# Seven block products in place of eight for the gate and value of the second block's FFNs

## The chip, the cores and the metric

The kernel runs on one core of one Trainium2 chip. The metric is the device time of one execution in microseconds, the median of several runs. TensorE (PE) multiplies, VectorE (DVE), ScalarE (ACT) and GpSimd (POOL) do elementwise work, and SyncE (SP) issues the loads of the weights.

## The reference, cut to what matters

Two blocks run one after the other on 512 tokens of 1024 channels, all in fp32. The first block (three mixers and a convolutional FFN) is not touched. The second block has a SwiGLU FFN ahead of its mixer and one behind it, and only these two are changed:

```
def swiglu(x, w_gate, w_up, w_down):
    return (jax.nn.silu(x @ w_gate) * (x @ w_up)) @ w_down

x = x + 0.5 * swiglu(rms_norm(x, ffn1_norm), ffn1_w_gate, ffn1_w_up, ffn1_w_down)
x = x + token_mixer(...)
x = x + 0.5 * swiglu(rms_norm(x, ffn2_norm), ffn2_w_gate, ffn2_w_up, ffn2_w_down)
```

The hidden width is 2816, which is 22 tiles of 128 channels.

## The kernel before

Activations lie with channels on the 128 partitions and the 512 tokens along the free dimension. A product of fp32 accuracy is made of three fp32r products: each operand is cut into a high part (ACT copies it with rounding, `whi`, `uh`, `hh`) and a low part (DVE subtracts, `wlo`, `ul`, `hl`), and PE adds up high by high, high by low and low by high (`dense`, L284).

All weights come in one stream, in tiles of 128 x 1024 fp32 (512 KB), in the order of use. `Weights.next` (L266 to L276) takes one: a load on SP's queue into `raw` (three buffers), the cut on ACT into `whi` (L273) and on DVE into `wlo` (L274), three buffers each.

In an FFN of the second block (`ffn2`, `glu`), a hidden tile j takes two weight tiles, gate and value. Each is eight input blocks of 128 by 128 against 512 tokens: 8 x 3 = 24 matmuls with a moving operand of 512 columns, so 48 for the two. The right side is `us`, x times the norm's vector and cut; the norm's factor by token, `R`, is multiplied in behind the product: `gg` = product x R (DVE), silu (ACT), x R (POOL, L1487), x value product (DVE, `gh`), then the cut into `hh` and `hl`. An FFN works in two halves of 11 hidden tiles, each followed by its part of the product with `w_down` (`down`), which adds into x (`xa` in the first FFN, `xb` in the second, called f1 and f2 here).

The products have six PSUM buffers (`mm`). The first three products of an FFN are made together by `first`, while x is still being finished. `R` comes from row sums on PE (`nst`), a power on POOL (`rr`), a spread by transposes on PE (`nbc`) and a copy on ACT (`R`).

The scheduler of the language sets the order of the instructions on each engine; each engine then works strictly in that order, waiting on semaphores.

Of the kernel before, what the change touches and what calls it, by code (L numbers as in the profile page):

```python
# [18 lines left out]
P = 128  # L19
T = 512  # L20
# [235 lines left out]
class Weights:  # L256
# [3 lines left out]
        self.nc, self.pool, self.src, self.raw_bufs, self.bufs = nc, pool, src, raw_bufs, bufs  # L260
        self.i = 0

    def next(self, label, e=None):
        nc, i = self.nc, self.i
        lab, bl = PLAN[i]
        assert lab == label, (lab, label)  # L266
        n = sum(len(c) for _, _, c in bl)
        raw = self.pool.tile([P, 1024], F32, name="raw", bufs=self.raw_bufs)
        nc.sync.dma_start(raw[:, :n], self.src[i][:, :n])
        w = raw[:, :n]  # L270
        hi = self.pool.tile([P, 1024], F32R, name="whi", bufs=self.bufs)
        lo = self.pool.tile([P, 1024], F32R, name="wlo", bufs=self.bufs)
        nc.scalar.activation(hi[:, :n], w, AF.Copy)  # L273
        (e or nc.vector).tensor_tensor(lo[:, :n], w, hi[:, :n].bitcast(F32), op=ALU.subtract)  # L274
        self.i += 1
        return hi, lo  # L276


# [1 line left out]
def two_blocks(ctx, tc, ins, out):  # L280
    nc = tc.nc
    S, V, G, PE = nc.scalar, nc.vector, nc.gpsimd, nc.tensor
# [24 lines left out]
    W = Weights(nc, wpool, ins["wst"], 3, 3)  # L307
# [28 lines left out]
    st = ctx.enter_context(tc.tile_pool(name="st", bufs=1))  # L336

    def tmp(name="tmp"):
        return st.tile([P, T], F32, name=name, tag="tmp", bufs=3)

    ALL = slice(0, T)
    HALVES = (slice(0, T // 2), slice(T // 2, T))
# [39 lines left out]
        return R  # L382

    class SqSum:
        def __init__(self, pool=None):
            self.acc = (pool or st).tile([P, T], F32, name="acc")
            self.new = {0, T // 2}

        def add(self, ap, e=V, s=ALL):
# [56 lines left out]
    part = big.tile([P, 8, T], F32, name="part")  # L446
# [5 lines left out]
    blk = ExitStack()  # L452
# [70 lines left out]
    with tc.tile_pool(name="lin", bufs=1) as lin, tc.tile_pool(name="p0", bufs=1, space=PSUM) as p0:  # L523
# [19 lines left out]
        mps, ws = [None] * 8, [None] * 8  # L543
# [66 lines left out]
    def pm():  # L610
        return bank("m", nm[0])
# [681 lines left out]
    R = st.tile([P, T], F32, name="R")  # L1293
# [64 lines left out]
    blk = ExitStack()  # L1358
    psm = blk.enter_context(tc.tile_pool(name="psm2", bufs=6, space=PSUM, reuse_waits="tile"))
    psx = blk.enter_context(tc.tile_pool(name="psx", bufs=2, space=PSUM, reuse_waits="tile"))  # L1360
    fp = blk.enter_context(tc.tile_pool(name="fp", bufs=1, reuse_waits="tile"))

    def pm():
        return psm.tile([P, T], F32, name="mm")
# [112 lines left out]

    k2, ka0, ka1, ka2 = sk

    def glu(label, R):  # L1480
        def hidden(j):
            pg = up(label)
            pv = up(label)
            g = fp.tile([P, T], F32, name="gg", bufs=3)
            tt(g, pg, R, MUL)
            act(g, g, AF.Silu)
            G.tensor_tensor(g, g, R, op=MUL)  # L1487
            h = fp.tile([P, T], F32, name="gh", bufs=2)
            tt(h, pv, g, MUL)
            return h  # L1490
        return hidden

    def ffn2(label, R, q):

        hidden = glu(label + "_up", R)
        for h in range(2):
            hs = []
            for j in range(11 * h, 11 * h + 11):
                t = hidden(j)
                a = fp.tile([P, T], F32R, name="hh", bufs=14)  # L1500
                b = fp.tile([P, T], F32R, name="hl", bufs=14)
# [43 lines left out]
    R = rms_bcast(pss, "pO", rn)  # L1545
# [123 lines left out]
    def pair(q, k, place):  # L1669

        h, l = parts(q, stage("h"), stage("l"))
        qs = [place("qa"), place("qb")]
        for s, o in enumerate(((h, l), (l, h))):
            for i in range(2):
                hand(qs[s][H2[i]], o[i][H2[s]])
        h, l = parts(k, stage("h"), place("kl"))
        ks = [place("ka"), place("kb")]
        for s, t in enumerate(ks):
            for i in range(2):
                hand(t[H2[i]], h[H2[s]])  # L1680
        return [(a, b, l) for a, b in zip(qs, ks)]
# [120 lines left out]
    with tc.tile_pool(name="cc", bufs=1, reuse_waits="tile") as cc:  # L1802
# [29 lines left out]
        for j in range(2):  # L1832
# [6 lines left out]
            for i in range(NB):  # L1839
                n = (i + 1) * P  # L1840
# [31 lines left out]
    ps = pT()  # L1872
# [178 lines left out]
```

## Time and profile before

| | |
|---|---|
| median of 3 runs | 2189.31 us (2188.54 to 2191.35) |
| the profiled execution | 2191.79 us, of which the span is 2190.0 us |
| PE busy, of the span | 97% |
| DVE, ACT, POOL busy | 52%, 36%, 23% |
| f1: from the first `gg` to the last add into `xa` | 935.3 to 1263.8 us |
| f2: from the first `gg` to the last add into `xb` | 1851.4 to 2186.3 us |

Times in the rows are microseconds from the start of the span. An engine's busy time is a union of its instructions; matmuls overlap each other, so the pace of PE is read from the distance of their starts, not from their durations. A number in square brackets behind a row is the engine's idle time ahead of it, with what ended it. "PEclk" is the granted TensorE clock as a share of full speed.

### The profile page before, as it was taken

The numbers are of one execution on the slowest core, as the hardware profiler recorded it, in microseconds if no ns is written. First come the engines' busy times: TensorE is split into PE (matmuls) and PEld (weight loads), VectorE is DVE, ScalarE is ACT, GpSimd is POOL, SyncE is SP. The second block draws the span as 40 slices with busy tenths as digits, with TensorE's granted clock in tenths as the row PEclk, the third lists the DMA queues.
The fourth block names the chain that finished last, engine by engine and source line by source line (L and its number), as shares of the span: only waits on it lengthen the run. The fifth ranks groups of instructions, "written<-read, shape, count | busy, mean of one in ns | idle before, by whom it ended". The sixth has DMA issues, their size and how long they took to land.

```text
span 2190.0 us, 31626 instructions
## 1 busy us (share of the span) xinstructions
PE 2132.7 (97%) x12492; PEld 1758.9 (80%) x12492; DVE 1145.0 (52%) x2158; ACT 787.1 (36%) x1330; POOL 513.5 (23%) x549
## 2 busy tenths in 40 slices
PE   7988999998999999899999999999999999999999
PEld 5877777666788888788888889998877888888887
DVE  6653445668652564643344439967554455433442
ACT  4422223553442443332222325445443233222221
POOL 3168661234000000321011023343121022100110
PEclk9988998998999999999999999999999999999999
DMA  8244334101452222222222343342252222222222
GB/s 309 100 137 155 118 132 135 52 11 45 160 176 98 99 99 97 68 95 97 97 97 96 124 147 107 94 139 78 104 151 77 97 96 96 97 96 96 97 97 86
DMA packets 84846, 238.31 MB, mean 109 GB/s; under 512 B 13970, under 2 KB 21448, under 8 KB 84570
## 3 DMA queue, kind: packets, MB, share of 16 engines
q1 hardware_dynamic: 78874, 226.19, 31.1%
q0 software_dynamic: 5104, 9.52, 1.2%
q8 instruction: 98, 1.61, 0.3%
q10 hardware_dynamic: 720, 0.57, 0.1%
q14 instruction: 50, 0.41, 0.1%
HBM read 216.02 MB, written 15.33 MB: 106 GB/s over the span
## 4 chain that ended last, share of the span: by engine, by line
PE 87%; POOL 4%; DMA 4%; DVE 3%; issue 1%; ACT 1%; SPq 0%; POOLq 0%; DVEq 0%; ACTq 0%
PE mm L284 67%; PE psm L284 4%; PE pS L284 3%; PE psr L284 2%; DMA raw<-in_ada_dram 2%; POOL am L634 2%; PE pO L284 2%; PE pss L284 2%; PE k L284 2%; PE pso L284 1%; POOL raw L633 1%; PE pT L1636 1%; PE pst L1097 1%; DMA raw<-in_wst_dram 1%; DVE ul L299 1%
## 5 line engine op out<-in xcount | busy, mean ns | idle before, releaser
L273 ACT ACTIVATE whi<-raw 128x1024 fp32r<-128x1024 f32 (+4 forms) x314 | 327.8, 1046 | 828.1 <-PE mm L284 608.5
L274 DVE TENSOR_TENSOR wlo<-raw,whi 128x1024 fp32r<-128x1024 f32 (+4 forms) x302 | 371.4, 1231 | 345.0 <-ACT whi L273 341.1
L284 PE MATMUL mm<-ul,whi 128*128 128x512 f32 (+1 forms) x1296 | 502.1, 388 | 6.0 <-DVE ul L299 6.0
L284 PE MATMUL mm<-uh,wlo 128*128 128x512 f32 (+1 forms) x1296 | 501.7, 388 | 1.0 <-DVE wlo L274 1.0
L284 PE MATMUL mm<-uh,whi 128*128 128x512 f32 (+1 forms) x1296 | 496.4, 388 | 4.3 <-ACT uh L287 3.3
L284 PEld LDWEIGHTS mm<-ul,whi 128*128 128x128 f32 x1296 | 245.1, 189 | 58.7 <-DVE ul L299 8.7
L284 PEld LDWEIGHTS mm<-uh,whi 128*128 128x128 f32 x1296 | 243.5, 190 | 55.4 <-ACT uh L287 4.7
L284 PEld LDWEIGHTS mm<-uh,wlo 128*128 128x128 f32 x1296 | 245.2, 189 | 51.1 <-DVE wlo L274 1.9
L284 PE MATMUL mm<-hh,wlo 128*128 128x512 f32 (+1 forms) x550 | 209.3, 381 | 0.0
L284 PE MATMUL mm<-hl,whi 128*128 128x512 f32 (+1 forms) x550 | 209.3, 381 | 0.0
L284 PE MATMUL mm<-hh,whi 128*128 128x512 f32 (+1 forms) x550 | 208.4, 381 | 0.0
L1487 POOL TENSOR_TENSOR gg<-gg,R 128x512 f32<-128x512 f32 x44 | 77.4, 1761 | 473.4 <-ACT gg L287 473.4
L284 PE MATMUL mm<-whi,uh 128*128 128x256 f32 (+1 forms) x488 | 140.5, 288 | 0.0
L284 PE MATMUL mm<-whi,ul 128*128 128x256 f32 (+1 forms) x488 | 139.8, 287 | 0.0
L284 PE MATMUL mm<-wlo,uh 128*128 128x256 f32 (+1 forms) x488 | 139.2, 285 | 0.0
L284 PEld LDWEIGHTS mm<-hl,whi 128*128 128x128 f32 x550 | 103.4, 188 | 19.9
L284 PEld LDWEIGHTS mm<-hh,whi 128*128 128x128 f32 x550 | 103.4, 188 | 19.8
L284 PEld LDWEIGHTS mm<-hh,wlo 128*128 128x128 f32 x550 | 103.4, 188 | 19.5
L287 ACT ACTIVATE p<-p,smin 128x128 f32<-128x128 f32 (+4 forms) x136 | 81.8, 602 | 91.8 <-DVE smin L1073 56.2
L290 DVE TENSOR_TENSOR gh<-mm,gg 128x512 f32<-128x512 f32 x44 | 30.4, 691 | 130.8 <-PE mm L284 125.2
L284 PEld LDWEIGHTS mm<-whi,ul 128*128 128x128 f32 x488 | 93.2, 191 | 1.7 <-issue 1.5
L284 PEld LDWEIGHTS mm<-whi,uh 128*128 128x128 f32 x488 | 93.0, 191 | 1.4 <-issue 0.4
(520 smaller groups left out, 3415.4 us busy)
## 6 DMA issues: line engine op xcount, KB each, us to landing
raw<-in_wst_dram SPq DMA_DIRECT2D x294, 512.0 KB, 3.2
raw<-in_ada_dram SPq DMA_DIRECT2D x32, 512.0 KB, 6.3
aw<-in_ada_dram SPq DMA_DIRECT2D x16, 512.0 KB, 8.5
raw<-in_wst_dram SPq DMA_DIRECT2D x8, 448.0 KB, 7.4
ka<-d POOLq DMA_DIRECT2D x1, 3570.0 KB, 49.9
k<-d POOLq DMA_DIRECT2D x1, 2556.0 KB, 20.8
part<-in_x_dram SPq DMA_DIRECT2D x4, 512.0 KB, 6.3
xa<-in_x_dram SPq DMA_DIRECT2D x8, 256.0 KB, 4.6
```

The lines of the kernel that those rows point to most:

```text
L273: nc.scalar.activation(hi[:, :n], w, AF.Copy)
L274: (e or nc.vector).tensor_tensor(lo[:, :n], w, hi[:, :n].bitcast(F32), op=ALU.subtract)
L284: PE.matmul(o, l, r, start=start, stop=stop)
L287: S.activation(o, i, f, **kw)
L290: V.tensor_tensor(o, a, b, op=op)
L299: V.scalar_tensor_tensor(o, a, s, b, op0=op0, op1=op1)
L633: G.tensor_scalar(aw[:, r], aw[:, r], s, 1.0, op0=MUL, op1=MUL)
L634: G.tensor_tensor(am, am, aw[:, r], op=ADD)
L1097: PE.transpose(ps[:, j:j + P], p[:, j:j + P], ident)
L1487: G.tensor_tensor(g, g, R, op=MUL)
L1636: PE.transpose(ps[:, j:j + P], p[:, o + j:o + j + P], ident)
```

## The change

Hidden tiles 0 to 2 of each FFN stay as they were. For tiles 3 to 21 the two weight tiles and the tokens are seen as two by two blocks: the left matrix has rows gate and value and columns channels 0 to 511 and 512 to 1023 (a11, a12, a21, a22, each 128 x 512 as stored); the right one has rows of channels and columns of tokens 0 to 255 and 256 to 511. Seven products of sums of blocks give the four blocks of outputs, where eight products of blocks did it before. One such product is 4 channel blocks x 3 = 12 matmuls with 256 moving columns; seven are 84.

- `Sevenths.make`, once for each FFN, builds the seven right sides for 4 channel blocks, cut into high and low (`th`, `tl`). It now takes R into them: 8 multiplications of 128 x 512 on DVE (`ta`, `tb`), 8 subtractions of 128 x 256 on POOL, 8 on DVE, 12 copies on ACT and 12 subtractions on DVE (256, 512 and 1024 wide). It works in two buffers in `part` (`stage`).
- `pair`, once for each of the 19 tiles, loads the two weight tiles, makes four sums of 128 x 512 on POOL (L1535 to L1538) into the same `stage` buffers, cuts three tiles of 1024 and one of 512 (`w4`), runs the products into three PSUM buffers (two of them are read by ACT or DVE part of the way and added to later), and makes up the outputs with five 256-wide operations on DVE and one addition on POOL (L1564), copies and silu on ACT. The last product of a tile (`rest`) is put behind the first of the next tile (`settle`).
- A `raw` buffer is now free for its next load when POOL's sums, ACT's copies and DVE's subtractions have all read it. In the built program the second weight tile of every pair (`w2`) gets the same one of the three buffers, and the first tiles (`w1`) take the other two by turns. `w2` is read by L1535 and L1537 on POOL, by ACT's copy into `w4h` and by DVE's subtraction into `w4l`, and on DVE's queue this `w4l` stands behind the two multiplications `gg<-gg,part` that finish the tile two before it.
- The buffers for `hh` and `hl` (14 each) become six and the free `us` slots; `gg` lies in a shared buffer.

```
+        def product(self, ps, a, c, which, start=False, stop=False):
+            for k in range(4):
+                ah, al = [w[:, c * T + k * P:c * T + k * P + P] for w in a]
+                bh, bl = [w[:, which] for w in self.t[k]]
+                for i, (l, r) in enumerate(((ah, bh), (ah, bl), (al, bh))):
+                    PE.matmul(ps, l, r, ...)
...
+        def pair(self, label, j, use):
+            w1, w2 = W.load(label), W.load(label)
+            a11, a12, a21, a22 = w1[:, :T], w1[:, T:], w2[:, :T], w2[:, T:]
+            s12, s34 = self.stage
+            G.tensor_tensor(s12[:, :T], a21, a22, op=ADD)
+            G.tensor_tensor(s12[:, T:], s12[:, :T], a11, op=SUB)
+            G.tensor_tensor(s34[:, :T], a11, a21, op=SUB)
+            G.tensor_tensor(s34[:, T:], a12, s12[:, T:], op=SUB)
+            wa, ws, wd = W.cut(w1), W.cut(s12), W.cut(s34)
+            wb = [fp.tile([P, T], F32R, name="w4" + c, bufs=2) for c in "hl"]
+            act(wb[0], a22, AF.Copy)
+            tt(wb[1], a22, wb[0].bitcast(F32), SUB)
...
+            self.product(pa_, wa, 0, 4, True)
+            act(s1, pa_, AF.Copy)
+            self.settle()
+            self.product(pb_, ws, 1, 1, True)
+            tt(u2, pb_, s1, ADD)
+            self.product(pc_, ws, 0, 0, True)
+            act(s5, pc_, AF.Copy)
+            self.product(pa_, wa, 1, 5, stop=True)
+            act(g[:, A], pa_, AF.Silu)
+            self.product(pb_, wd, 0, 2)
+            tt(u3, pb_, s1, ADD)
+            self.product(pc_, wd, 1, 6, stop=True)
+            tt(g[:, B], pc_, u2, ADD)
+            act(g[:, B], g[:, B], AF.Silu)
+            G.tensor_tensor(s5, s5, u3, op=ADD)
+            def rest():
+                self.product(pb_, wb, 0, 3, stop=True)
+                tt(s1, pb_, s1, ADD)
+                tt(g[:, B], g[:, B], s5, MUL)
+                tt(g[:, A], g[:, A], s1, MUL)
+                use(g)
+            self.owed = rest
...
     def ffn2(label, name, R, q, seven):
         hidden = glu(label + "_up", R)
+        seven.make(name, R)
         for h in range(2):
...
             for j in range(11 * h, 11 * h + 11):
+                if j < S0:
+                    use(hidden(j))
+                else:
+                    seven.pair(label + "_up", j, use)
```

At the start of f1, DVE's queue before the change goes from the spread of the norm (`rv`, `rb`) at once to the first `gg`, with the weights' cuts between:

```order
L294 TENSOR_SCALAR rv<-nst 128x4
L373 COPY rb<-rr 128x512
L274 TENSOR_TENSOR wlo<-raw,whi 128x1024
L290 TENSOR_TENSOR gg<-mm,R 128x512 x3
L290 TENSOR_TENSOR gh<-mm,gg 128x512
```

The same queue after the change, the last twelve rows up to the first `gg`; `ta`, `tb` and `part` are `make`'s operands, `tl` the low cuts of the right sides:

```order
L305 SCALAR_TENSOR_TENSOR tb<-xa_4300,vec,R 128x512
L296 TENSOR_TENSOR part<-tb,part 128x256
L296 TENSOR_TENSOR tl_8449<-part,th_8448 128x1024
L296 TENSOR_TENSOR tl_8453<-ta,th_8452 128x256
L305 SCALAR_TENSOR_TENSOR ta<-xa_4297,vec,R 128x512
L296 TENSOR_TENSOR tl_8453<-tb,th_8452 128x512
L296 TENSOR_TENSOR tl_8451<-part,th_8450 128x1024
L296 TENSOR_TENSOR part<-tb,part 128x256
L296 TENSOR_TENSOR tl_8455<-ta,th_8454 128x256
L305 SCALAR_TENSOR_TENSOR tb<-xa_4301,vec,R 128x512
L296 TENSOR_TENSOR part<-tb,part 128x256 x2
L296 TENSOR_TENSOR gg<-mm,R 128x512
```

Between `rb` and the first `gg` there now stand 24 instructions of `make`: 8 of form `ta` or `tb`, 11 of 128 x 256, 3 of 128 x 512 and 2 of 128 x 1024; behind this `gg` come a subtraction of 256, a cut of 512, a `gg` and a cut of 1024. The first block product stands on PE 12 matmuls (all 512 wide) behind `nbc` in f1 and 40 behind it in f2, and needs a PSUM buffer that the first `gg` frees, since tiles 0 to 2 hold all six.

On POOL, before the change, the queue of f1 holds one multiplication for each hidden tile:

```order
L396 TENSOR_TENSOR acc<-acc,sq 128x512 x7
L362 TENSOR_TENSOR rr<-rv,mhalf 128x4
L1487 TENSOR_TENSOR gg<-gg,R 128x512 x22
L274 TENSOR_TENSOR wlo<-raw,whi 128x1024 x3
L362 TENSOR_TENSOR rr<-rv,mhalf 128x4
```

After the change these five rows repeat, tile after tile (the sixth is the next tile's first); the addition L1564 belongs to a tile two before that of the sums around it:

```order
L1535 TENSOR_TENSOR part<-raw 128x512
L1564 TENSOR_TENSOR part<-part 128x256
L1536 TENSOR_TENSOR part<-part,raw 128x512
L1537 TENSOR_TENSOR part<-raw 128x512
L1538 TENSOR_TENSOR part<-raw,part 128x512
L1535 TENSOR_TENSOR part<-raw 128x512
```

POOL thus has four 512-wide and one 256-wide operation for a tile, where it had one of 512.

## Rows read from the trace of the kernel before

**Rows 1.** The page: engines' busy time, and the chain that ended last by engine.

```profile
PE 2132.7 (97%) x12492; PEld 1758.9 (80%) x12492; DVE 1145.0 (52%) x2158; ACT 787.1 (36%) x1330; POOL 513.5 (23%) x549
...
PE 87%; POOL 4%; DMA 4%; DVE 3%; issue 1%; ACT 1%; SPq 0%; POOLq 0%; DVEq 0%; ACTq 0%
```

**Rows 2.** Windows of f1, two hidden tiles; columns: stretch, us, busy by engine, PEclk, DMA.

```profile
937.00:947.88 10.88, 10.88 (x49) 9.01 (x48) 7.85 (x10) 5.18 (x8) 6.43 (x4) 1.00 0.23 78
947.88:958.76 10.88, 10.88 (x49) 9.01 (x48) 4.44 (x5) 3.19 (x4) 1.81 (x1) 1.00 0.35 116
```

**Rows 3.** Timeline of PE, 256-column matmuls at 882.7 us; columns: start, us, instruction.

```profile
882.72 0.28 PE L284 MATMUL mm<-hh,wlo 128*128 128x256 f32 x1
882.84 0.28 PE L284 MATMUL mm<-hh,whi 128*128 128x256 f32 x1
...
883.80 0.28 PE L284 MATMUL mm<-hh,wlo 128*128 128x256 f32 x1
```

**Rows 4.** Timelines of POOL and DVE, 918 to 928 us, both engines on SBUF operands.

```profile
919.25 2.15 POOL L396 TENSOR_TENSOR acc<-acc,sq 128x512 f32<-128x512 f32 x1
918.10 6.62 DVE L274 TENSOR_TENSOR wlo<-raw,whi 128x1024 fp32r<-128x1024 f32 x3 [2.79 <-ACT whi L273]
926.49 1.23 DVE L274 TENSOR_TENSOR wlo<-raw,whi 128x1024 fp32r<-128x1024 f32 x1 [1.77 <-ACT whi L273]
```

**Rows 5.** Timelines of POOL and DVE at 1854.7 us; the DVE operation reads PSUM.

```profile
1854.66 1.30 POOL L1487 TENSOR_TENSOR gg<-gg,R 128x512 f32<-128x512 f32 x1
1854.73 0.69 DVE L290 TENSOR_TENSOR gh<-mm,gg 128x512 f32<-128x512 f32 x1 [2.03 <-POOL gg L1487]
```

**Rows 6.** Timelines of ACT and PE: `R`, and `nbc` with the matmul behind it, f1 and f2.

```profile
934.69 0.60 ACT L287 ACTIVATE R<-nbc 128x512 f32<-128x512 f32 x1 [2.10 <-PE nbc L376]
934.41 0.47 PE L284 MATMUL mm<-uh,whi 128*128 128x512 f32 x1
1850.78 0.60 ACT L287 ACTIVATE R<-nbc 128x512 f32<-128x512 f32 x1 [0.97 <-PE nbc L376]
1850.50 0.48 PE L284 MATMUL mm<-uh,wlo 128*128 128x512 f32 x1
```

**Rows 7.** Timeline of DVE: 512-wide with three operands, and 256-wide operations.

```profile
519.11 0.74 DVE L299 SCALAR_TENSOR_TENSOR tmp<-xa,gf,R 128x512 f32<-128x512 f32 x1
519.77 0.74 DVE L299 SCALAR_TENSOR_TENSOR xa<-tmp,sg,xa 128x512 f32<-128x512 f32 x1
906.20 0.41 DVE L1457 TENSOR_TENSOR tmp<-part,R 128x256 f32<-128x256 f32 x1
906.53 0.96 DVE L299 SCALAR_TENSOR_TENSOR ul<-xa,vec,uh 128x256 fp32r<-128x256 f32 x1
908.21 0.47 DVE L299 SCALAR_TENSOR_TENSOR ul<-xa,vec,uh 128x256 fp32r<-128x256 f32 x1
```

**Rows 8.** Timeline of POOL: 256-wide, and two 512-wide that follow each other.

```profile
906.42 0.80 POOL L1457 TENSOR_TENSOR tmp<-part,R 128x256 f32<-128x256 f32 x1 [0.43 <-DVE xa L299]
936.76 1.29 POOL L1487 TENSOR_TENSOR gg<-gg,R 128x512 f32<-128x512 f32 x1 [7.50 <-ACT gg L287]
938.02 1.30 POOL L1487 TENSOR_TENSOR gg<-gg,R 128x512 f32<-128x512 f32 x1
```

**Rows 9.** Groups by line of f1, 937 to 1278 us; columns: xcount, busy us, mean ns, idle before.

```profile
L274 DVE TENSOR_TENSOR wlo<-raw,whi 128x1024 fp32r<-128x1024 f32 x58 | 71.5, 1233 | 45.7 <-ACT whi L273 45.7
L273 ACT ACTIVATE whi<-raw 128x1024 fp32r<-128x1024 f32 x61 | 64.7, 1061 | 214.4 <-PE mm L284 195.1 <-issue 18.8 <-ACT uh L287 0.6
L1487 POOL TENSOR_TENSOR gg<-gg,R 128x512 f32<-128x512 f32 x22 | 39.1, 1781 | 233.5 <-ACT gg L287 233.5
L290 DVE TENSOR_TENSOR hl<-gh,hh 128x512 fp32r<-128x512 f32 x22 | 15.6, 708 | 0.0
L290 DVE TENSOR_TENSOR gg<-mm,R 128x512 f32<-128x512 f32 x20 | 13.8, 690 | 49.2 <-PE mm L284 49.2
```

**Rows 10.** DMA issues of f1, 936 to 1200 us: count, size, median us to landing.

```profile
raw<-in_wst_dram SPq DMA_DIRECT2D x48, 512.0 KB, 3.1
```

**Rows 11.** Windows around the start of f1, where PE waits; columns as in rows 2.

```profile
888.00:891.00 3.00, 0.71 (x7) 0.47 (x5) 2.11 (x4) 1.63 (x3) 1.19 (x1) 1.00 0.53 175
891.00:902.00 11.00, 8.31 (x39) 7.96 (x40) 10.06 (x23) 3.74 (x8) 3.74 (x5) 0.53 0.15 48
```

More of the change, by code (lines that the diff above doesn't have):

```diff
@@ L261, in __init__, with load @@
         self.i = 0
-    def next(self, label, e=None):
+    def load(self, label):
         nc, i = self.nc, self.i
@@ L269, in next, with cut @@
         nc.sync.dma_start(raw[:, :n], self.src[i][:, :n])
-        w = raw[:, :n]
+        self.i += 1
+        return raw[:, :n]
+    def next(self, label, e=None):
+        return self.cut(self.load(label), e)
+    def cut(self, w, e=None):
+        nc, n = self.nc, w.shape[-1]
         hi = self.pool.tile([P, 1024], F32R, name="whi", bufs=self.bufs)
@@ L274, in next @@
         (e or nc.vector).tensor_tensor(lo[:, :n], w, hi[:, :n].bitcast(F32), op=ALU.subtract)
-        self.i += 1
         return hi, lo
@@ L384, in two_blocks, with __init__ @@
     class SqSum:
-        def __init__(self, pool=None):
-            self.acc = (pool or st).tile([P, T], F32, name="acc")
+        def __init__(self, pool=None, tag=None):
+            self.acc = (pool or st).tile([P, T], F32, name="acc", **(dict(tag=tag, bufs=2) if tag else {}))
             self.new = {0, T // 2}
@@ L1360, in two_blocks @@
     psx = blk.enter_context(tc.tile_pool(name="psx", bufs=2, space=PSUM, reuse_waits="tile"))
-    fp = blk.enter_context(tc.tile_pool(name="fp", bufs=1, reuse_waits="tile"))
+    fp0 = ExitStack()
+    fp = fp0.enter_context(tc.tile_pool(name="fp", bufs=1, reuse_waits="tile"))
     def pm():
@@ L1478, in two_blocks, with __init__, make, settle @@
     k2, ka0, ka1, ka2 = sk
+    S0 = 3
+    class Sevenths:
+        def __init__(self):
+            fp.tile([P, 16], F32, name="pad0")
+            self.t = [[fp.tile([P, 7, 256], F32R, name=f"t{c}{k}") for c in "hl"] for k in range(4)]
+            fp.tile([P, 48], F32, name="pad1")
+            self.stage = [part[:, 4 * i:4 * i + 2].rearrange("p a b -> p (a b)") for i in range(2)]
+            self.snap = [[part[:, 4 * i + 2 + c // 2, c % 2 * 256:c % 2 * 256 + 256] for c in range(4)] for i in range(2)]
+            self.owed = None
+        def make(self, name, R):
+            A, B = HALVES
+            for k in range(4):
+                ta, tb = tmp("ta"), tmp("tb")
+                stt(ta, x[k], vc(name, k), R, MUL, MUL)
+                stt(tb, x[k + 4], vc(name, k + 4), R, MUL, MUL)
+                t = self.stage[k % 2].rearrange("p (a b) -> p a b", b=256)
+                G.tensor_tensor(t[:, 0], ta[:, B], ta[:, A], op=SUB)
+                G.tensor_tensor(t[:, 2], tb[:, B], ta[:, B], op=SUB)
+                tt(t[:, 1], tb[:, B], t[:, 0], SUB)
+                tt(t[:, 3], tb[:, A], t[:, 1], SUB)
+                h, l = self.t[k]
+                b2 = tb.rearrange("p (a b) -> p a b", b=256)
+                for i, v in ((slice(4, 5), ta[:, None, A]), (slice(5, 7), b2), (slice(0, 4), t)):
+                    act(h[:, i], v, AF.Copy)
+                    tt(l[:, i], v, h[:, i].bitcast(F32), SUB)
+        def product(self, ps, a, c, which, start=False, stop=False):
+            for k in range(4):
+                ah, al = [w[:, c * T + k * P:c * T + k * P + P] for w in a]
+                bh, bl = [w[:, which] for w in self.t[k]]
+                for i, (l, r) in enumerate(((ah, bh), (ah, bl), (al, bh))):
+                    PE.matmul(ps, l, r, start=start and k == i == 0, stop=stop and k == 3 and i == 2,
+                              skip_group_check=True)
+        def settle(self):
+            if self.owed:
+                self.owed()
+                self.owed = None
+        def pair(self, label, j, use):
[10 more added lines that the diff above has]
+            tt(wb[1], a22, wb[0].bitcast(F32), SUB)
+            n = slice(0, 256)
+            A, B = HALVES
+            s1, s5, u2, u3 = self.snap[j % 2]
+            g = tmp("gg")
+            pa_ = pm()[:, n]
+            self.product(pa_, wa, 0, 4, True)
+            act(s1, pa_, AF.Copy)
+            self.settle()
+            pb_ = pm()[:, n]
+            self.product(pb_, ws, 1, 1, True)
+            tt(u2, pb_, s1, ADD)
+            pc_ = pm()[:, n]
+            self.product(pc_, ws, 0, 0, True)
[15 more added lines that the diff above has]
+            self.owed = rest
@@ L1483, in hidden @@
             pv = up(label)
-            g = fp.tile([P, T], F32, name="gg", bufs=3)
+            g = tmp("gg")
             tt(g, pg, R, MUL)
@@ L1487, in hidden, with ffn2, use @@
             G.tensor_tensor(g, g, R, op=MUL)
-            h = fp.tile([P, T], F32, name="gh", bufs=2)
-            tt(h, pv, g, MUL)
-            return h
+            tt(g, pv, g, MUL)
+            return g
         return hidden
-    def ffn2(label, R, q):
+    def ffn2(label, name, R, q, seven):
         hidden = glu(label + "_up", R)
+        seven.make(name, R)
         for h in range(2):
             hs = []
[L1498 to L1501, printed above, removed]
+            def use(t):
+                j = 11 * h + len(hs)
+                i = j - 6 if j < 14 else j - 17 if j > 19 else -1
+                if i < 0:
+                    a, b = [fp.tile([P, T], F32R, name="hh" if c == "h" else "hl", bufs=6) for c in "hl"]
+                else:
+                    a, b = two(i)
                 act(a, t, AF.Copy)
@@ L1504, in ffn2 @@
                 hs.append((a, b))
+            for j in range(11 * h, 11 * h + 11):
+                if j < S0:
+                    use(hidden(j))
+                else:
+                    seven.pair(label + "_up", j, use)
+            seven.settle()
             def done(m, ps, s):
@@ L1512, in two_blocks @@
     first("f1_up", halves=HF, e=V)
-    q = SqSum(fp)
+    fp0.close()
+    fp = blk.enter_context(tc.tile_pool(name="fp1", bufs=1, reuse_waits="tile"))
+    seven = Sevenths()
+    q = SqSum(fp, "w4h")
     for k in range(8):
@@ L1523, in f1_done @@
             nc.sync.dma_start(xd[m], x[m])
-    ffn2("f1", R, f1_done)
+    ffn2("f1", "f1n", R, f1_done, seven)
     blk.close()
@@ L2000, in two_blocks @@
     fp = blk.enter_context(tc.tile_pool(name="fp4", bufs=1, reuse_waits="tile"))
+    seven = Sevenths()
     first("f2_up", lambda *a: raw("f2n", *a))
     R = rms_bcast(psx, "px", rms_rows(psx, "px", q.acc))
-    ffn2("f2", R, lambda m, s: nc.sync.dma_start(out[m], x[m]))
+    ffn2("f2", "f2n", R, lambda m, s: nc.sync.dma_start(out[m], x[m]), seven)
     blk.close()
```

## The prediction

> **What bounds the kernel now.** The page comes first: PE is busy for 97% of the span and carries 87% of the chain that ended last [rows 1], so time is gained where PE does less, and lost where PE is made to wait. The second view is the windows of the changed stretch: one hidden tile takes 10.88 us, PE is busy in all of it at the full granted clock, and the others have room (second window: DVE 4.44, ACT 3.19, POOL 1.81) [rows 2]. 10.88 over 48 matmuls is 0.2267 us for one of 512 columns. The third is the timeline at the end of the first block's FFN, where matmuls of 256 columns run with nothing in between: nine of them in 1.08 us, 0.120 each [rows 3]. A half-wide matmul thus costs 53% of a full one, not 50%.
>
> **PE's work.** A changed tile takes 84 x 0.120 = 10.08 us in place of 10.88: 0.80 saved, and 38 x 0.80 = 30.4 us for 19 tiles in each FFN, if PE never waits. The Trainium skill, "TensorE: Matmul & The Clock Gate", section "Back-to-back issue gap", gives 518 and 262 cycles for these two widths; by that estimate the saving would be 1.19 us a tile, 45 in all. The rows decide here.
>
> **What POOL and DVE do to each other.** Three cuts `wlo` beside POOL's additions took 6.62 us, 2.21 each, where one alone took 1.23; the addition in between took 2.15 where two in a row start 1.26 apart [rows 4, 8]. 2.21 is about one of each after the other: they take turns. A DVE operation that reads PSUM took 0.69 beside a POOL operation of 1.30, so nothing was added to either [rows 5]. I therefore let every DVE operation on two SBUF operands and every POOL operation exclude each other. What a cut of 1024 adds to POOL's path is 2.21 - 1.26 = 0.95; for 512 I take half, 0.47, for 256 a quarter, 0.24 (estimates). The Trainium skill, "SBUF — State Buffer", section "Who interferes with whom", has this as a rule: a DVE instruction with two SBUF inputs contends with a GpSimd instruction that reads SBUF, and whoever starts first blocks the other. It speaks against this change, and the rows agree with it; without it the sum is that of the third rival.
>
> **A tile in the steady state.** The second weight tiles use one buffer, so a loop goes round once a tile: load 3.1 [rows 10], POOL's four sums 4 x 1.26 = 5.04 and its 256-wide addition 0.80 [rows 8], and DVE operations that get their turn in between: one `wlo` 0.95, the two multiplications that stand ahead of `w4l` 0.48, and `w4l` itself 0.47, behind which the load may start. The sum is 10.84. That is above PE's 10.08 and almost the old 10.88: such a tile gains 0.04. PE should be seen waiting for the 256-wide addition on PSUM that stands behind `w4l` on DVE. Lower end: if `w4l` gets its turn before POOL's fourth sum, the loop is 9.6 and PE's 10.08 holds. Upper end: one more `wlo` in POOL's path, 11.79. I take the middle, since all four sums stand without a gap in POOL's queue. I count 5 tiles of an FFN at PE's pace (three in the first half, whose loads have a lead or whose waits are counted below; two in the second, loaded during `down`), 14 in the loop: 5 x 0.80 + 14 x 0.04 = 4.6 us gained, 9.2 for both.
>
> ACT has by `pair` three copies of 1024 at 1.06 [rows 9] and about 3 us of small ones in a tile, 6 of 10: no bound. Its copies stay in the shade, unless a cut waits for a buffer.
>
> **The start of each FFN.** `make` can't begin before R. On DVE 25 instructions stand from there to the first `gg`, which frees the PSUM buffer for the first block product: 8 x 0.66 (their starts in a row), 11 x 0.33, 3 x 0.63, 2 x 1.15 and 0.69 [rows 7, 9], the starts of the last three forms taken 0.08 before the end of the one ahead, as in rows 7: 13.8 us. POOL's eight subtractions take their turns in between; one of them stretched a DVE operation from 0.47 to 0.96 [rows 7], so 8 x 0.49 = 3.9. Together 17.7 (13.8 if they exclude nothing).
>
> In f1, R is done at 935.3 and PE then has 12 matmuls of 512 from 934.4, to 937.1 [rows 6]. The first block product comes at 935.3 + 17.7 = 953.0: PE idles 15.9 us. In f2, R is done at 1851.4, PE has 40 matmuls from 1850.5 to 1859.6 [rows 6], the product comes at 1869.1: 9.5 idle.
>
> Then the first tile's sums. They need the buffer that `make` still reads: from the first `gg` on DVE 0.33 + 0.63 + 0.61 + 1.15 = 2.7 us. On POOL the sum L1535, a `gg`, L1537 and L1536 follow, 4 x 1.26, with one cut of 1024 and two of 512 taking turns, 0.95 + 0.94; then ACT's copy 1.06: 10.7 in all, of which PE fills 24 x 0.12 = 2.9. Idle: 7.8 us. After that DVE owes five cuts of 1024 beside POOL's sums, 2.21 each, where a product takes PE 1.44: 5 x 0.77 = 3.9.
>
> So f1 loses 15.9 + 7.8 + 3.9 = 27.6, f2 21.2: 48.8. Nothing hides it; before the change the multiplication by R stood behind the products and PE ran on.
>
> **The clock.** Where PE waited at 888 to 891 us (busy 0.71 of 3.0), the granted share was 0.53 from 891 to 902, the 1.2 GHz level for most of it [rows 11]. Idle stretches of 8 to 16 us should do the same. What of such a stretch falls into waiting costs nothing; at worst all 11 us are work at half pace, 5.5 lost for each FFN. I take 3 each, 6.
>
> **Sum.** +48.8 - 9.2 + 6 = +45.6 us. The profiled execution took 2191.8 (span 2190.0), so it would become 2237.4; the median lies 2.5 below it. On the median, 2189.3 + 45.6 = 2235 us, slower by 2.1%.
>
> **Rivals.**
> - The loop is heavier: one more `wlo` in POOL's path makes 11.79 of the 10.84, and 28 tiles x 0.95 = 26.6: 2262. For it: DVE has three `wlo` in every tile. Against: during the 3.1 us of the load POOL does nothing, and two of them fit there.
> - The loop doesn't bind: `w4l` wins its turn. All 38 tiles at PE's pace: 2189.3 + 48.8 + 6 - 30.4 = 2214. For it: PE's tile order leaves the queues room for 2.9 us between the products concerned; against: rows 4, where POOL came back after each single cut.
> - Not slower: POOL's and DVE's operations here don't exclude each other, since other operands lie in other places than in rows 4. Then the start is 13.8 long, PE idles 12.0 and 5.6, then 2.7 + 5.0 + 1.06 - 2.9 = 5.9 in each, nothing for the cuts: 29.4 against 30.4 saved, 2188. That is the tie; idle under 26 us in all would make it faster by over 0.2%. For it: rows 5 show that the exclusion depends on where operands lie. Against: rows 4 are the same forms on SBUF tiles of other names.
> - The change not doing what it says: the scheduler could have left PE's order as it was. The program's order shows 84 matmuls of 256 for a tile, so I give it nothing.
>
> **How the numbers follow.** Forecast 72%, heavier loop 11%, loop not binding 9%, no exclusion 8%. The forecast's own range is 2216 to 2256: 11 us for `make` and the first sums (8 x 0.49 twice, and 1.5 for each start), 6 for the clock. The range for 8 in 10 reaches up past the heavier loop to 2266 and down below the lighter to 2209, and leaves out the tie. A measurement of this kernel can tell about 0.2%, 4.4 us, from no change. Faster by more: 0.03, from the tie's lower side; within it 0.04; slower 0.93.
>
> **What would show it.** In the profile after: an idle PE of some 16 us behind the norm in f1 and 9 in f2, both ended by DVE (a `gg` or a low cut of `make`), then one of some 8 ended by ACT's `whi<-part`; half clock close by; tiles at 10.8 us with one wait of 0.7 or so in each; `wlo` with a mean well above 1.23, and POOL's sums above 1.26. If the tiles run at 10.1, the loop was wrong; if the first idle is under 10 in f1, the start was; if `wlo` stays at 1.23, the exclusion.

## The result

The changed kernel takes 2248.0 us (2246.68 to 2249.87) against 2188.93 (2188.41 to 2191.35) before: a ratio of 1.0268, 95% interval 1.025 to 1.0286. It is slower by 59 us; forecast were 46, with 2235 us in a range of 2209 to 2266.

The profiled execution took 2247.27 us, its span 2245.5. The two lines of the page that stood in [rows 1]: PE's busy share fell from 97% to 94%. The second line can't be set beside the 87% of before as it stands: the chain is followed back only to 911.7 us here, and its shares add up to 60% of the span. Of that stretch (1330 us) the chain lies on PE for 69%, where from 912 us on it was 98% before; "issue" and DVE have about a tenth each now, the DMA and POOL a twentieth each.

```profile
PE 2109.4 (94%) x13860; PEld 1799.3 (80%) x13860; DVE 1385.8 (62%) x2442; ACT 886.0 (39%) x1544; POOL 736.7 (33%) x717
...
PE 41%; issue 6%; DVE 6%; DMA 3%; POOL 3%; ACT 1%; POOLq 0%; SPq 0%; DVEq 0%; ACTq 0%
```

PE is busy for 2109 us, 23 less than before, and yet the span is 55 longer: the work fell and the waiting grew. From the end of `R` to the last add into x, f1 went from 329.2 to 361.1 us and f2 from 335.6 to 362.1, together +58.4; what lies between them is unchanged (586.9 and 587.3). So the whole loss sits in the two changed stretches. The span grew by 55 and not by 58.4 because `R` of f1 was done 3.3 us earlier in this execution (931.96 in place of 935.28); in the profiles of the variants below that time lies anywhere from 931.6 to 936.6.

**The start.** The timeline of PE, the matmuls with the longest idle times ahead of them and a short one, f1 and then f2. Before, PE did not wait at this place at all [rows 6].

```profile
950.02 0.55 PE L1523 MATMUL mm<-th,whi 128*128 128x256 f32 x1 [15.93 <-DVE gg L296]
...
962.17 0.58 PE L1523 MATMUL mm<-th,whi 128*128 128x256 f32 x1 [5.94 <-ACT whi L280]
963.84 0.58 PE L1523 MATMUL mm<-th,wlo 128*128 128x256 f32 x1 [0.45 <-DVE wlo L281]
1898.90 0.55 PE L1523 MATMUL mm<-th,whi 128*128 128x256 f32 x1 [10.02 <-DVE gg L296]
...
1911.72 0.58 PE L1523 MATMUL mm<-th,whi 128*128 128x256 f32 x1 [5.97 <-ACT whi L280]
```

The first idle stretch ends with the first `gg` on DVE, behind `make`; the second with ACT's copy of the first summed weight tile. In f1, `R` is done at 931.96, and DVE's queue then shows 17.2 us of `make` without a hole up to that `gg`:

```profile
931.99 0.75 DVE L305 SCALAR_TENSOR_TENSOR ta<-xa,vec,R 128x512 f32<-128x512 f32 x1 [4.46 <-ACT R L293]
...
948.00 1.28 DVE L296 TENSOR_TENSOR part<-tb,part 128x256 f32<-128x256 f32 x2
949.20 0.68 DVE L296 TENSOR_TENSOR gg<-mm,R 128x512 f32<-128x512 f32 x1
```

The windows behind it show the granted clock (PEclk, third from the end of a row; the first two rows are means over stretches at both levels). Where PE works from 950 to 966 us, the granted share is 0.50 and the half-wide matmuls start 0.21 us apart, the 1.2 GHz level; then 0.118.

```profile
949.20:960.00 10.80, 5.74 (x24) 5.27 (x24) 10.70 (x14) 5.90 (x10) 9.01 (x6) 0.66 0.00 0
960.00:971.00 11.00, 7.96 (x49) 7.47 (x50) 10.14 (x7) 5.19 (x7) 9.68 (x6) 0.72 0.30 95
971.00:982.00 11.00, 10.02 (x86) 9.84 (x84) 8.34 (x10) 3.90 (x7) 8.69 (x6) 1.00 0.36 116
```

**The tiles behind it.** In the loop PE waits once a tile, for a DVE operation that reads PSUM:

```profile
1002.93 0.39 PE L1523 MATMUL mm<-th,whi 128*128 128x256 f32 x1 [1.53 <-DVE part L296]
1014.35 0.38 PE L1523 MATMUL mm<-th,whi 128*128 128x256 f32 x1 [1.26 <-DVE part L296]
```

The two rows stand 11.42 us apart; over the 27 such tiles the mean is 11.37, where a tile took 10.88 before [rows 2]. The chain of waits of this tile, in order of time (start, us, what), shows the round:

```profile
1000.77 1.78 DVE w4l L296
...
1002.62 3.56 DMA raw<-in_wst_dram
...
1006.31 0.04 POOL part L1535
...
1007.57 1.72 POOL part L1564
...
1010.75 0.42 DVE part L296
...
1012.18 0.84 DVE w4l L296
```

The chain counts only a part of the last `w4l`; the whole of it stands in DVE's timeline:

```profile
1012.18 1.77 DVE L296 TENSOR_TENSOR w4l<-raw,w4h 128x512 fp32r<-128x512 f32 x1
```

`w4l` frees the buffer, the load runs, POOL's first sum starts 3.8 us behind the end of `w4l`, and 7.6 us later the next `w4l` ends. The groups of the stretch 1140 to 1200 us (columns as in [rows 9]) show who stretches whom:

```profile
L281 DVE TENSOR_TENSOR wlo<-part,whi 128x1024 fp32r<-128x1024 f32 x12 | 14.7, 1224 | 3.8 <-ACT whi L280 3.8
L296 DVE TENSOR_TENSOR gg<-gg,part 128x256 f32<-128x256 f32 x10 | 12.8, 1285 | 3.3 <-POOL part L1564 3.2
L1564 POOL TENSOR_TENSOR part<-part 128x256 f32<-128x256 f32 x6 | 10.5, 1757 | 0.0
L296 DVE TENSOR_TENSOR w4l<-raw,w4h 128x512 fp32r<-128x512 f32 x5 | 8.9, 1778 | 0.0
L1537 POOL TENSOR_TENSOR part<-raw 128x512 f32<-128x512 f32 x5 | 7.4, 1475 | 0.0
L296 DVE TENSOR_TENSOR part<-mm,part 128x256 f32<-128x256 f32 x16 | 6.6, 411 | 0.0
```

A 256-wide product takes 1.285 us and a 512-wide cut 1.778, though a 256-wide DVE operation took 0.41 and a 512-wide one 0.71 before [rows 7, 9]; POOL's 256-wide addition takes 1.757 where 0.80 were seen [rows 8]. The operation that reads PSUM takes 0.411, also where it lies beside POOL (at 1010.75). The cut of 1024 keeps its 1.22 on average: two of a tile's three run while POOL waits for the load, and beside the third it is POOL's L1564 that gets longer. So the mean of one group isn't enough to see the exclusion.

### The profile page after: what moved, and what is told of

It is laid out like the page before. It is cut to its first block, busy times and chain, and to the rows that moved or that the text cites. A ratio compares the mean times of both kernels' runs of the same rounds, so it can differ in the third digit from the quotient of the medians.

```text
span 2245.5 us, 35288 instructions
## 1 busy us (share of the span) xinstructions
PE 2109.4 (94%) x13860; PEld 1799.3 (80%) x13860; DVE 1385.8 (62%) x2442; ACT 886.0 (39%) x1544; POOL 736.7 (33%) x717
## 4 chain that ended last, share of the span: by engine, by line
PE 41%; issue 6%; DVE 6%; DMA 3%; POOL 3%; ACT 1%; POOLq 0%; SPq 0%; DVEq 0%; ACTq 0%
PE mm L290 29%; PE mm L1523 5%; DMA raw<-in_wst_dram 3%; PE pS L290 3%; POOL part L1564 2%; DVE w4l L296 2%; PE pO L290 2%; PE pT L1745 1%; DVE part L296 1%; DVE tl L296 1%; DVE wlo L281 1%; DVE gg L296 1%; PE pT L1728 1%; ACT whi L280 1%; PE pT L290 0%
## 5 line engine op out<-in xcount | busy, mean ns | idle before, releaser
L290 PE MATMUL mm<-ul,whi 128*128 128x512 f32 (+1 forms) x848 | 327.8, 388 | 8.0 <-DVE ul L305 8.0
L1523 PE MATMUL mm<-th,whi 128*128 128x256 f32 x912 | 259.5, 288 | 76.0 <-DVE part L296 36.7
L290 PE MATMUL mm<-uh,wlo 128*128 128x512 f32 (+1 forms) x848 | 327.3, 387 | 0.5 <-DVE wlo L281 0.5
L290 PE MATMUL mm<-uh,whi 128*128 128x512 f32 (+1 forms) x848 | 321.6, 387 | 4.7 <-ACT uh L293 3.4
L1523 PE MATMUL mm<-tl,whi 128*128 128x256 f32 x912 | 255.2, 283 | 0.0
L1523 PE MATMUL mm<-th,wlo 128*128 128x256 f32 x912 | 247.9, 284 | 1.3 <-DVE wlo L281 1.3
L1523 PEld LDWEIGHTS mm<-th,whi 128*128 128x128 f32 x912 | 175.3, 192 | 84.4 <-DVE part L296 41.3
L290 PEld LDWEIGHTS mm<-uh,whi 128*128 128x128 f32 x848 | 158.6, 189 | 38.6 <-ACT uh L293 4.8
L1523 PEld LDWEIGHTS mm<-tl,whi 128*128 128x128 f32 x912 | 175.4, 192 | 0.2
L1523 PEld LDWEIGHTS mm<-th,wlo 128*128 128x128 f32 x912 | 170.8, 192 | 2.3 <-DVE wlo L281 2.3
L1535 POOL TENSOR_TENSOR part<-raw 128x512 f32<-128x512 f32 x38 | 54.3, 1429 | 211.5 <-DMA raw<-in_wst_dram 151.1
```

The source lines that it names most:

```text
L290: PE.matmul(o, l, r, start=start, stop=stop)
L1523: PE.matmul(ps, l, r, start=start and k == i == 0, stop=stop and k == 3 and i == 2, skip_group_check=True)
L1535: G.tensor_tensor(s12[:, :T], a21, a22, op=ADD)
```

## The experiments

Each is a change to the changed kernel unless it says otherwise; times are medians. The kernel before took 2191.39 us beside E1 to E4 and 2190.47 beside E5 to E8.

**E1, a fourth weight buffer.** Is it the one buffer of `w2`, or the turns of POOL and DVE, that sets a tile? `load` with a pool given takes a tile `rawb` from it.

```
-            w1, w2 = W.load(label), W.load(label)
+            w1, w2 = W.load(label), W.load(label, j % 2 and fp)
...
-                i = j - 6 if j < 14 else j - 17 if j > 19 else -1
+                i = j - 5 if j < 13 else j - 18 if j > 17 else -1
...
-                    a, b = [fp.tile([P, T], F32R, name="hh" if c == "h" else "hl", bufs=6) for c in "hl"]
+                    a, b = [fp.tile([P, T], F32R, name="hh" if c == "h" else "hl", bufs=5) for c in "hl"]
```

> The changed kernel with a fourth weight buffer: the second weight tile of every odd hidden tile is loaded into a buffer of its own, so that no load has to wait for the tile just before it (the buffers for the cut hidden values become five, to make room). In the changed kernel's trace a tile in the loop takes 11.4 us, of which 3.4 to 3.8 lie between the end of `w4l` and the first sum on POOL (the load).
>
> Theory of turns (mine): POOL's sums and DVE's operations on two SBUF operands exclude each other, and their own sum is the bound. From the rows of the changed kernel: POOL 4 x 1.26 + 0.80 = 5.84, DVE 3 x 1.14 (cuts) + 0.61 + 0.60 + 2 x 0.33 = 5.29, together 11.1 us a tile. The load then is no longer waited for, but the tile stays at 11.1: 28 tiles x 0.3 = 8 us faster than the changed kernel, 2240 us (2230 to 2248).
>
> Theory of the buffer: the round of the one buffer alone sets the pace. Without it PE sets it, at 84 x 0.117 = 9.8 us a tile: 28 x 1.6 = 45 us faster, 2203 us.

Measured: 2236.92 us, 11 less than the changed kernel, where the turns gave 8 and the buffer 45. POOL no longer waits for a DMA; it waits for a cut on DVE, and PE for the same DVE operation as ever. The groups of POOL's first two sums (1140 to 1200 us), and PE's timeline:

```profile
L1539 POOL TENSOR_TENSOR part<-part,raw 128x512 f32<-128x512 f32 x6 | 13.7, 2283 | 0.0
...
L1538 POOL TENSOR_TENSOR part<-rawb 128x512 f32<-128x512 f32 x3 | 3.9, 1301 | 11.5 <-DVE wlo L284 11.5
```

```profile
1150.21 0.38 PE L1526 MATMUL mm<-th,whi 128*128 128x256 f32 x1 [1.15 <-DVE part L299]
1161.15 0.38 PE L1526 MATMUL mm<-th,whi 128*128 128x256 f32 x1 [1.15 <-DVE part L299]
```

A tile takes 10.94 us, 0.2 under the 11.1 to which all turns add up; that sum is an estimate, and it is not reached in full. Taking the load out of the round gained 0.43 us a tile, no more: without it, DVE's cuts of 1024 that stood in its shade fall into POOL's path (L1539 goes to 2.28).

**E2, the sums on DVE.** The same five operations (L1535 to L1538, L1564), on the engine that is already the busier one.

```
-            G.tensor_tensor(s12[:, :T], a21, a22, op=ADD)
+            V.tensor_tensor(s12[:, :T], a21, a22, op=ADD)
...
-            G.tensor_tensor(s5, s5, u3, op=ADD)
+            V.tensor_tensor(s5, s5, u3, op=ADD)
```

> The changed kernel with the four sums of a tile and the addition L1564 on DVE in place of POOL; nothing else. DVE is the busier engine: 9.6 of 11 us in the windows of the changed kernel's loop.
>
> Theory of turns: what DVE gets in addition, 4 x 0.60 + 0.33 = 2.7 us a tile, is less than what POOL's operations take from the shared access (5.84). DVE's queue comes to 5.3 + 2.7 + four operations on PSUM of 0.34 = 9.4 us a tile, under PE's 9.8: the waits of 1.1 to 1.7 us in each tile go, 41 us in all, and of the 7.6 and 8.3 us ahead of the first tile's second product some 2 each: 2205 us (2198 to 2215).
>
> Rival, no exclusion: DVE's 9.6 of 11.4 are its own work, and 2.7 more make 12.3 us a tile: 28 x 0.9 = 25 us slower than the changed kernel, 2273 us.

Measured: 2203.85 us, 44 less than the changed kernel. Behind the start the tiles run 9.89 us apart in both FFNs, with hardly a wait. The waits ahead of the first tile's second product fell by only some 0.5 us each, where 2 were expected. The groups of the same stretch:

```profile
L281 DVE TENSOR_TENSOR wlo<-part,whi 128x1024 fp32r<-128x1024 f32 x12 | 14.6, 1221 | 0.6
...
L296 DVE TENSOR_TENSOR gg<-gg,part 128x256 f32<-128x256 f32 x12 | 5.0, 418 | 0.0
...
L296 DVE TENSOR_TENSOR w4l<-raw,w4h 128x512 fp32r<-128x512 f32 x6 | 4.1, 684 | 0.0
L1535 DVE TENSOR_TENSOR part<-raw 128x512 f32<-128x512 f32 x6 | 4.1, 683 | 0.0
L1564 DVE TENSOR_TENSOR part<-part 128x256 f32<-128x256 f32 x7 | 2.9, 417 | 0.0
```

The product went from 1.285 to 0.418 and `w4l` from 1.778 to 0.684, with nothing changed in them. A sum takes 0.683 on DVE against 1.26 and more on POOL. In the window 1140 to 1200 us (the changed kernel first, then E2; the third busy time is DVE's, the fifth POOL's) PE is busy throughout in E2. DVE was busy for 51.8 of 60 us and now is for 57.5, but more tiles pass in that time: it comes to 9.8 us a tile before and 9.5 now. With five operations more DVE works less on a tile than with POOL beside it, since part of its busy time was waiting inside its operations. (`pair` has six 256-wide operations on DVE, four that read PSUM and two products; the text on the change counts five.)

```profile
1140.00:1200.00 60.00, 53.91 (x454) 52.90 (x453) 51.77 (x60) 28.32 (x48) 37.49 (x27) 1.00 0.31 102
1140.00:1200.00 60.00, 60.00 (x512) 60.00 (x511) 57.50 (x98) 34.17 (x55) 0.00 (x0) 1.00 0.34 107
```

**E5, E1 with one cut less on DVE.** Does DVE's length reach PE through the turns, with POOL's work untouched?

```
-            wa, ws, wd = W.cut(w1), W.cut(s12), W.cut(s34)
+            wa, ws = W.cut(w1), W.cut(s12)
+            hi = W.pool.tile([P, 1024], F32R, name="whi", bufs=3)
+            act(hi, s34, AF.Copy)
+            wd = hi, ws[1]
```

> E1 (four weight buffers, sums on POOL) without one of DVE's three cuts of 1024 in each changed tile: the low part of the third cut tile is left out and that of the second taken for it, so the output is not the reference's. POOL's work is untouched.
>
> Theory of turns: in E1 the tile took 11.0 us, the sum of POOL's 5.84 and DVE's 5.29 on two SBUF operands. With 1.14 less on DVE the sum is 9.98, just above PE's 9.8: 28 tiles x 1.0 = 28 us less than E1, 2209 us (2203 to 2216).
>
> Rival, POOL's own chain is the bound in E1 (its operations 5.84 and the waits for the operands of L1564 between them): DVE's cut is off it, and the time stays at E1's 2237, within 5 us.

Measured: 2208.27 us, 29 less than E1. Most tiles stand 9.95 to 9.97 apart. So DVE's cut was on the path, and POOL's own chain is not the bound in E1. It is no test of the sum of the turns (9.98) to a tenth: in this window PE shows no wait any more, DVE waits 4.2 us of the 60 for PE, and 9.97 lies only 0.08 above PE's own 9.89.

```profile
1140.00:1200.00 60.00, 60.00 (x508) 59.96 (x508) 48.81 (x62) 33.62 (x55) 36.77 (x30) 1.00 0.33 106
```

**E7, E2 with additions on POOL that nobody reads.**

```
+            for v, u in ((a11, a21), (a12, a22)):
+                G.tensor_tensor(fp.tile([P, T], F32, name="idle"), v, u, op=ADD)
```

> E2 (all sums on DVE) with two additions of 128 x 512 for each changed tile put back on POOL, of the same halves of the weight tiles as before, into a buffer that nobody reads. Nothing waits for their results; a weight buffer waits until they have read it.
>
> Theory of turns: they take the access to SBUF from DVE for 2 x 1.26 us a tile. DVE's operations on two SBUF operands are 5.3 + 2.7 = 8.0, so the two together come to 10.5, and to 11.9 if none of DVE's 1.4 us on PSUM lies beside POOL: I take 11.2 against E2's 9.8, for some 34 tiles: 48 us slower than E2, 2252 us (2228 to 2275).
>
> Rival, E2 was faster only because DVE's sums are shorter and nothing waits for POOL any more: as E2, 2204 us, within 5.

Measured: 2245.51 us, 42 more than E2, for work that no instruction waits for but the reload of a buffer. The groups (1140 to 1200 us):

```profile
L281 DVE TENSOR_TENSOR wlo<-part,whi 128x1024 fp32r<-128x1024 f32 x11 | 16.7, 1515 | 0.0
L1540 POOL TENSOR_TENSOR idle<-raw 128x512 f32<-128x512 f32 x10 | 15.3, 1525 | 42.4 <-DMA raw<-in_wst_dram 42.0
...
L1566 DVE TENSOR_TENSOR part<-part 128x256 f32<-128x256 f32 x5 | 5.8, 1164 | 0.0
L1535 DVE TENSOR_TENSOR part<-raw 128x512 f32<-128x512 f32 x5 | 5.6, 1110 | 0.5 <-DMA raw<-in_wst_dram 0.5
```

Against E2, DVE's addition L1566 went from 0.417 to 1.164 and its sum L1535 from 0.683 to 1.110: what stands beside POOL's two operations pays for them. DVE waited 0.5 us for a DMA in these 60 us, so the weight buffers are not the reason. As in E1 and E5 there are five `hh` and `hl` buffers in place of six; E5 runs at 9.97 us a tile with them, so they are not the reason either. Some 5 of the 42 us came by way of the clock: behind three of PE's waits of 1.9 to 2.2 us the granted share was 0.50 for 3.4 us each. E2 and E7 together settle the exclusion: one takes POOL's operations away, the other puts some back without any use, and the time follows both ways.

**E6, `make` alone.**

```
-    S0 = 3
+    S0 = 22
...
-            self.t = [[fp.tile([P, 7, 256], F32R, name=f"t{c}{k}") for c in "hl"] for k in range(4)]
+            self.t = [[fp.tile([P, 7, 256], F32R, name=f"t{c}{k}") for c in "hl"] for k in (0, 1, 0, 1)]
...
+                a, b = [fp.tile([P, T], F32R, name="hh" if c == "h" else "hl", bufs=11) for c in "hl"]
```

> `make` alone: S0 = 22, so that every hidden tile keeps the old form and no product reads what `make` builds; `make` stands where it stood. (Its four right sides share two sets of buffers, to leave room for eleven `hh` and `hl`.)
>
> Theory of the start: DVE reaches the first `gg` only behind `make`, some 17.5 us after R, and PE, out of PSUM buffers, waits 16 us in f1 and 10 in f2 as in the changed kernel; then half clock, some 3 us in each. The 7.7 and 8.3 us ahead of the first tile's second product are absent: before + 26 + 6 = 2221 us (2213 to 2227).
>
> Rival, the start's loss comes from the first sums and cuts of the changed tiles and not from `make`: within 5 us of the kernel before.

Measured: 2222.03 us, 32 more than before, 1 from the forecast. PE waits 15.6 us in f1, as in the changed kernel, and 11.9 in f2, where that has 10.0. The wait ahead of the first matmul that needs a PSUM buffer, and the end of the slow clock (f1):

```profile
953.03 0.77 PE L290 MATMUL mm<-uh,whi 128*128 128x512 f32 x1 [15.59 <-DVE gg L296]
953.59 0.63 PE L290 MATMUL mm<-ul,whi 128*128 128x512 f32 x1
...
958.71 0.63 PE L290 MATMUL mm<-ul,whi 128*128 128x512 f32 x1
959.14 0.43 PE L290 MATMUL mm<-uh,wlo 128*128 128x512 f32 x1
959.41 0.40 PE L290 MATMUL mm<-uh,whi 128*128 128x512 f32 x1
```

Matmuls of 512 start 0.43 us apart until 959.1 and 0.23 after it.

**E3, two more old tiles to cover `make`.**

```
-    S0 = 3
+    S0 = 5
...
-        seven.make(name, R)
...
+                if j == 3:
+                    seven.make(name, R)
```

> The changed kernel with hidden tiles 3 and 4 in the old form as well (S0 = 5), and `make` written behind the first three tiles, so that two old tiles, 2 x 10.88 us of PE's work, lie beside it. The loop is left as it is; two tiles fewer go through it in each FFN.
>
> Theory of the start: the idle stretches of PE at the start (16.1 + 7.7 in f1, 10.2 + 8.3 in f2 in the changed kernel, 43 us with the small ones) and 9 us at the lower clock are the wait for `make`. With 21.8 us of work beside it, on the DVE that also has these tiles' operations (some 14 us) to do, I expect 15 of idle left in f1 and 9 in f2, and half of the clock's loss: 2248 - 19 - 5 = 2224 us (2215 to 2234). That the two tiles each leave the loop changes little (11.4 against 10.88).
>
> Rival, the start is not the cause (POOL's and DVE's work is only moved, and PE waits later for the same length): within 5 us of 2248.

Measured: 2225.26 us, 23 less than the changed kernel. In f1 the first wait fell from 15.9 to 3.5 us (in f2 from 10.0 to 5.4), but the one ahead of the first summed weight tile did not go; in f1 it grew from 5.9 to 8.1:

```profile
962.17 0.58 PE L1523 MATMUL mm<-tl,whi 128*128 128x256 f32 x1 [3.51 <-DVE tl L296]
...
974.42 0.58 PE L1523 MATMUL mm<-th,whi 128*128 128x256 f32 x1 [8.05 <-ACT whi L280]
```

So two tiles cover most of `make`, but not the first sums behind it.

**E4, both cures, and E8 with one more tile in the new form.**

```
-    S0 = 3
+    S0 = 7
...
-                G.tensor_tensor(t[:, 0], ta[:, B], ta[:, A], op=SUB)
+                V.tensor_tensor(t[:, 0], ta[:, B], ta[:, A], op=SUB)
...
+                if 3 <= j < 7:
+                    seven.make(name, R, j - 3)
```

`make` now does one of its four parts at a call; its other subtraction on POOL and the five operations of E2 go to DVE as well. E8 has S0 = 6 and the parts ahead of tiles 2 to 5.

> Both cures together, meant to beat the kernel before: sums, addition and the eight subtractions of `make` on DVE, S0 = 7, and `make` in four parts, one ahead of each of the hidden tiles 3 to 6.
>
> Theory of turns and of the start: PE has 43.5 us of old tiles beside `make`, DVE needs about 41 for both, so PE waits 0 to 5 us at each start and not in the loop. 15 tiles in each FFN save 10.88 - 9.8 = 1.08: 32 us off the kernel before, with 0 to 10 lost: 2157 to 2170, I take 2165 us.
>
> Rival, no exclusion: the loop's tiles get longer than the old ones by DVE's work, 12.3 against 10.88: 30 x 1.4 = 42 us slower than the kernel before, 2230 us or more.

> E4 with S0 = 6 and the parts of `make` ahead of the hidden tiles 2 to 5: one more tile of each FFN in the new form, and 10.88 us less of old work beside `make`.
>
> Theory of the start: 2 x 1.08 = 2.2 us more are saved; DVE needs about 41 us for `make` and six old tiles' work less what is done before R, PE has 32.6 + 2.7 in f1 and 32.6 + 9.1 in f2, so 2 to 6 us of waiting come back in f1 and little in f2: 2167 + 2 = 2169 us (2163 to 2174).
>
> Rival, `make` is covered by less than that: 2165 us, as E4 with one tile more.

Measured: E4 takes 2166.98 us, a ratio of 0.9887 to the kernel before (0.9866 to 0.9908): faster than both kernels, by 24 and by 81 us. E8 takes 2171.31 (0.9914, 0.9899 to 0.9929). PE's waits at the start, measured as distances of starts beyond the pace, come to 1.7 and 1.5 us in E4, to 5.5 and 2.9 in E8, and there are none later. The intervals of E4 and E8 overlap, so which of the two is better is not shown. In E4's windows of the cover (`make` beside old tiles), the change of form and the first tiles, PE has no hole but a short one, and DVE is the engine without room:

```profile
938.20:981.00 42.80, 42.80 (x191) 35.45 (x190) 41.86 (x63) 22.29 (x32) 9.22 (x6) 1.00 0.21 74
982.00:994.00 12.00, 10.67 (x87) 10.22 (x87) 11.38 (x15) 5.97 (x9) 2.23 (x1) 1.00 0.38 133
994.00:1014.00 20.00, 20.00 (x172) 20.00 (x172) 19.31 (x34) 11.18 (x19) 0.00 (x0) 1.00 0.40 128
```

## Why the prediction was right, and where its sizes were off

The sign, the two places and the mechanisms held; the sum was 13 us short. By its own terms, for both FFNs, against the profiled executions:

| term | predicted | measured |
|---|---|---|
| PE idle at the starts | +48.8 | +43.3 |
| half clock | +6 | +9.4 |
| PE's saving, 38 tiles | -30.4 | -37.6 |
| waits in the loop | +21.2 | +41.3 |
| sum | +45.6 | +56.4 |

The measured terms are sums over PE's timeline (distances of starts beyond the pace); 2 of the 58.4 us are spread over smaller distances. The faster pace stands in two rows: it adds 7.2 us to the saving and, under a round of the same length, 28 x 0.19 = 5.3 to the waits. The shorter idle times (5.5) were offset by the clock and the small distances (5.4), and that is luck.

- **`make`** was right within 0.3 us in f1 and 0.7 in f2: predicted 17.7 from `R` to the end of the first `gg`, measured in f1 931.96 to 949.88, 17.9; PE idle 15.9 and 9.5 predicted, 16.1 and 10.2 measured as distances. E6 shows this term by itself.
- **The first tile's sums**: 7.8 predicted, 7.7 and 8.3 measured. The term behind it, 3.9 for each FFN while DVE makes up its cuts, was too large: 0.6 and 0.5. PE ran at half clock just there, so DVE had the time that the term denied it; that one loss was counted in both terms is likely, but no run shows it. The clock's own was put too low (3 for each; 4.2 and 5.3).
- **PE's pace.** A tile takes 9.89 us where nothing holds it (E2, E4), not 10.08: these 256-wide matmuls start 0.118 us apart, those of [rows 3] 0.120. By an estimate from the 262 cycles that the Trainium skill, "TensorE: Matmul & The Clock Gate", section "Back-to-back issue gap", gives for 256 columns, it would be 9.2 us; the rows of E2 decide against it.
- **The loop is the step that failed.** It was put at 10.84 us and took 11.37; over some 28 tiles that is 15 us; the other errors nearly cancel, and 13 were missing. The term that was mis-sized is the load. It was taken as 3.1 us [rows 10]; between the end of `w4l` and the first sum lie 3.5 to 3.9 in nearly every tile of the loop. There the next tile's first load is issued 2.1 us behind it, while before loads came one each 5.4 us; whether this is the cause was not tried. The rest of the round was right: 7.74 predicted, 7.65 from the start of the first sum to the end of `w4l`. What the prediction did not work out is the bound that lies just behind this one: it counted along POOL's path and let two cuts of 1024 lie under the load, but did not add up what POOL and DVE need of the shared access in one tile. That sum, 5.84 + 5.29 = 11.1, was to be had from the same rows and lies above 10.84. In the changed kernel the round with its load is longer (11.37) and sets the pace; with the load out of the round the tile stays at 10.94 (E1), still above the 10.84, and it falls with DVE's part (E5).
- **The exclusion** was right (E2, E7), and PSUM operands are exempt (0.411 beside POOL, 0.42 without). The Trainium skill, "SBUF — State Buffer", section "Who interferes with whom", says that a DVE instruction with two SBUF inputs contends with a GpSimd instruction that reads SBUF, and that the order of issue decides who blocks. The traces agree with the first, with `w4l` at 1.78 beside POOL's sums and 0.68 without them; the second fits the `w4l` of 1012.18, which starts 0.24 us behind POOL's L1538 and ends 0.54 behind its end. But the sign by which the prediction would have known it was badly chosen: the mean of `wlo` stayed at 1.22 in the loop. The cost moved to the operations that happen to stand beside POOL's.
- **The rivals.** The heavier loop (2262) came nearer in the loop than the forecast did, 11.37 being in the middle between 10.84 and 11.79, but not by its mechanism: not one more `wlo` but the longer load made the difference. The lighter loop fell with the distances in the loop, the tie without exclusion with E2 and E7. That tie was also worked out without the 6 us of the clock, though PE idles 12.0 and 5.6 us in it; with them it comes to 2194, beyond the 4.4 us that were to count as no change.

## What to carry to other kernels

Where POOL and DVE share an access, add up what both need of it in one round, as for one engine, and compare that with the bound; do this beside the longest path, not in place of it. An addition that POOL does in 1.26 us and DVE in 0.68 then belongs on DVE even where DVE looks busy, since part of that busy time is waiting for POOL; what counts is DVE's own work, 9.5 us of a tile of 9.89 in E2. And a preparation that can only start when a late value is known needs about as much old work beside it as it is long. Both together turned a loss of 59 us into a gain of 24: the sums on DVE gave 44 (E2), and four old tiles more per FFN, with `make` in parts and its POOL operations on DVE, the other 37 (E4).

## What the runs showed of the hardware

- Additions on POOL that nothing waits for cost 42 us (E7): two of 1.26 us in 38 tiles are 96 us of POOL's time, so 44% of it reached the end, some 5 us by way of the clock.
- With the fourth buffer (E1) the exclusion only changes its victims: `w4l` stays at 1.78, the cut `wlo<-part` goes from 1.22 to 1.41 and POOL's second sum from 1.29 to 2.28, while L1564 falls from 1.76 to 0.74.
- After PE had stood for 15.6 us (E6), matmuls ran at the 1.2 GHz level for 6.1 us (granted share 0.50), 14 of 512 columns at 0.43 us: 2.9 us lost.
